# A small cast moved behind a split, other places for first weights, products in three passes, and a norm's small steps issued first

## The chip, the cores and the metric

The kernel runs on one core of one Trainium2 chip, as a single launch. The metric is the device time in microseconds (us) of the whole program; before the change it is 1896.98 us, the median of three runs.

## The reference

A decoder trunk of two layers over 512 tokens of width 1024, all in float32. Each layer is four blocks, each followed by a layer norm over the residual sum (a is a constant):

```python
x = layer_norm(a * x + 0.5 * swiglu_ffn(x, ffn_w_in[i, 0], ffn_w_out[i, 0]), ...)
h = diff_attention(...) if i == 0 else pool_mixer(...)
x = layer_norm(a * x + h, ...)
x = layer_norm(a * x + memory_cross_attention(x, mem, ...), ...)     # 256 memory tokens
x = layer_norm(a * x + 0.5 * swiglu_ffn(x, ffn_w_in[i, 1], ffn_w_out[i, 1]), ...)

def swiglu_ffn(x, w_in, w_out):          # w_in 1024 x 5632, w_out 2816 x 1024
    g, u = jnp.split(x @ w_in, 2, axis=-1)
    return (jax.nn.silu(g) * u) @ w_out
```

There are thus four feed-forward blocks, called blocks 1 to 4 below, and eight norms.

## The kernel before

Every float32 product is made of three matmuls. An operand is split into a high part (a cast on ACT, the ScalarE) and the rest (a subtraction on DVE, the VectorE): `xh`, `xl` for activations, `wh`, `wl` for weights. `mm3` multiplies high by high (L232), then L233 and L234 for the two mixed terms. The residual X stands in four tiles of 128 tokens, called X_76 to X_79 in the order of instructions; they are turned by TensorE through PSUM (`pt`), and cast and split into `xh` and `xl`.

A feed-forward block multiplies 2x2 blocks by seven products instead of eight. Its first half, `up()`, works on three column groups at a time ("lanes" 0, 1 and 2), in turns. A lane loads the raw weights `ra` and `rc` (later `rd`), some with an accumulating load issued on POOL, splits each in `operand()` (cast L769, subtraction L771), and makes the products x, y and z in PSUM; DVE combines them (L847) and ACT copies what has to be kept (`sp`, L832). A product that stands first for its block (`by_passes`, L796) takes 24 matmuls; before the change these are eight pairs on `xh` and `xl` with the weight's high part, and eight on `xh` with its low part.

A split weight lies in one of three kinds of place: the two turning buffers `wh`/`wl`, and two long places named `above` and `below`, which the mixers use too. `hl()` chooses by a counter:

```python
self.slot += self.by_fours
if self.by_fours and self.slot % 4 < 2:
    return self.long_place(self.slot % 2, shape, False)     # 0: above, 1: below
# else: the next buffer of wh and wl
```

The norm of a token tile (`ln_token`) is: partial sums with the residual on DVE (L397), mean on DVE (L406), Square with a running sum on ACT (L414), `var` on ACT (L415), `rstd` on POOL (L416), and two steps over the tile on DVE (L418, L420). `second_factors` then makes sums of turned tiles for the seven products (`hb`, L728 and L706).

The order on each engine is set by the order in the program text together with priorities (`high_priority`, `issue_after`, `behind`); each engine then runs its list in that order. `da_constants` prepares the attention's constants beside block 1: the mask is loaded by SP late, behind the block's last weights, cast to bfloat16 by DVE (L1829), and a gain is scaled (L1830). `left_over` is what remains of the last h's split in block 1 (L919 its low part).

Of the kernel before, what the change touches and what calls it, by code (L numbers as in the profile page):

```python
# [12 lines left out]
AF = mybir.ActivationFunctionType  # L13
ALU = mybir.AluOpType
# [4 lines left out]
D = 1024  # L19
S = 512  # L20
NT = S // P
# [6 lines left out]
EPS = 1e-5  # L28
# [4 lines left out]
LAM_INIT = 0.8 - 0.6 * math.exp(-0.3 * 0)  # L33
# [15 lines left out]
    scale=0.8,  # L49
# [78 lines left out]
class Trunk:  # L128
# [272 lines left out]
    def ln_token(self, t):  # L401
        nc, X = self.nc, self.X[t]
        g, b = self.ln_gb
        s = self.ln_sums[t]
        mean, var, rstd = (self.small(n, (P, 1)) for n in ("mean", "var", "rstd"))
        nc.vector.tensor_scalar(mean, s[:, 0:1], s[:, 1:2], -1.0 / D, ALU.add, ALU.mult)  # L406
        if self.last_ln:
            cols = [slice(half * S, (half + 1) * S) for half in range(2)]
        else:
            cols = [slice(0, D)]  # L410
        g, b = ([x[:, c] for c in cols] for x in (g, b))
        y = [X[:, c] for c in cols]
        sq = self.act(self.spare, (P, D), mybir.dt.bfloat16)
        square = nc.scalar.activation(sq, X, AF.Square, bias=mean, accum_out=var)  # L414
        nc.scalar.activation(var, var, AF.Copy, scale=1.0 / D, bias=EPS * self.ln_scale**2)  # L415
        nc.gpsimd.tensor_tensor(rstd, var, self.mhalf[:, 0:1], ALU.pow)  # L416
        for i, c in enumerate(cols):
            begin = nc.vector.scalar_tensor_tensor(y[i], X[:, c], mean, g[i], ALU.add, ALU.mult)  # L418
        for i, c in enumerate(cols):
            end = nc.vector.scalar_tensor_tensor(X[:, c], y[i], rstd, b[i], ALU.mult, ALU.add)  # L420
            if self.last_ln:
                nc.sync.dma_start(self.out[t * P : (t + 1) * P, c], X[:, c])
        self.ends.append((square, end))
        self.begins = square, begin
        self.passes.append(begin)
        if t == NT - 1:
            self.gates = list(self.next_gates)
        if self.make_xt:
            self.late.append(t)
# [157 lines left out]
    def ffn(self, layer, j, ln, beside=()):  # L587
        w_in, w_out = self.a["ffn_w_in"][layer, j], self.a["ffn_w_out"][layer, j]
        self.seven_of, self.factors = {}, self.factor_tiles()
        self.slot, self.by_fours, self.alike, self.urgent = 0, True, False, False  # L590
        nc, n, beside = self.nc, len(FFN_TURNS), iter(beside)
        at_start = bool(self.load_rest)
        downs = {i: self.down(d, w_out, 2.0 * ALPHA if i == 1 else 1.0) for i, (_, d) in enumerate(FFN_TURNS) if d}
# [152 lines left out]
    def up(self, w, u, lane, early, between):  # L746
# [5 lines left out]
        nc, H = self.nc, 2 * P  # L752
# [5 lines left out]
        def load(tag, *block):  # L758
            t = self.raw_tile((4, H), tag)
            self.last_load = nc.sync.dma_start(t, source(*block))  # L760
            return t
# [4 lines left out]
        def operand(raw, *behind):  # L766
            v = self.hl([P, 4, H])
            with self.after([act for act, _ in behind]):
                hi = nc.scalar.copy(v[0], raw)  # L769
            with self.after([dve for _, dve in behind]):  # L770
                lo = nc.vector.tensor_sub(v[1], raw, v[0].bitcast(F32))  # L771
            splits.append((hi, lo))
            return v

        def product(ps, v, a, start=False, passes=False):
            if passes or between and start and a == 0:
                by_passes(ps, v, a)
                return
            x = self.factors[a]
            for j in range(2):  # L780
                o = slice(j * P, (j + 1) * P)
                for k in range(4):

                    self.mm3(
                        ps[:, j], (v[0][:, k, o], v[1][:, k, o]), (x[0][:, k], x[1][:, k]),
                        start and j == k == 0, j == 1 and k == 3, True,
                    )

        def by_passes(ps, v, a, which=range(3)):

            x = self.factors[a]
            halves = [(n, i, l) for n in range(8) for i, l in ((0, 0), (0, 1))]
            for group in ([halves[:8], halves[8:], [(n, 1, 0) for n in range(8)]][w] for w in which):
                for n, i, l in group:
                    j, k = divmod(n, 4)
                    self.last_mm = nc.tensor.matmul(  # L796
                        ps[:, j], v[i][:, k, j * P : (j + 1) * P], x[l][:, k],
                        start=n == i == l == 0, stop=n == 7 and i == 1, skip_group_check=True,
                    )
# [5 lines left out]
        at_start = early > 0 and self.begins is None  # L805
# [7 lines left out]
        v = operand(ra, *((self.turned_parts,) if third and at_start else ()))  # L813
# [6 lines left out]
        if at_start and lane == 0:  # L820
            by_passes(x, v, 0, (0,))
            yield
# [4 lines left out]
        if at_start and lane == 0:  # L827
            by_passes(x, v, 0, (1, 2))
        else:
            product(x, v, 0, True, third and at_start)  # L830
# [19 lines left out]
        if not at_start or lane == 1:  # L850
            v = operand(ra)
            if u == FFN_LAST[1]:
                with self.tc.issue_after(splits[-1][1].ins):
                    self.left_over()
        elif third:
            v = operand(ra, self.made_parts, self.factor_parts)
        else:
            v = operand(ra, self.made_parts)
            self.made_parts = splits[-1]
            yield  # L860
# [6 lines left out]
        rd = load("rc", 2, 2)  # L867
# [3 lines left out]
        p5 = sp()  # L871
        nc.scalar.copy(p5, z)
        yield
        v = operand(rd)
        if at_start and lane == 0:
            self.made_parts = splits[-1]
            yield
# [14 lines left out]
        s = self.tmp("sp", (P, 2, H))  # L892
# [923 lines left out]
    def da_constants(self):  # L1816
        nc, a = self.nc, self.a
        c = lambda shape, name, dt=F32: self.ropep.tile(shape, dt, name=name)
        self.rope = c([P, 2], "rope")
        nc.sync.dma_start(self.rope, a["rope"])  # L1820
        self.ropeC, self.ropeS = c([P, S], "ropeC"), c([P, S], "ropeS")
        m = self.ropeC[:, :P]
        self.subg = c([P, 1], "subg")
        with self.tc.issue_after(self.last_load.ins):
            nc.sync.dma_start(m, a["mask"])
            nc.sync.dma_start(self.subg, a["da_subln_g"].rearrange("a p -> p a"))
        yield
        self.maskr = c([P, P], "maskr", mybir.dt.bfloat16)
        nc.vector.tensor_copy(self.maskr, m)  # L1829
        nc.vector.tensor_scalar(self.subg, self.subg, 1.0 - LAM_INIT, None, ALU.mult)  # L1830
        yield from self.rope_tables()


# [27 lines left out]
```

## Time and profile before

| | |
|---|---|
| median of three runs | 1896.98 us (1894.94 to 1900.29) |
| profiled execution, its own time | 1896.17 us |
| its span in the trace | 1894.4 us |
| busy: TensorE, its weight loads | 1880.5 us, 1779.3 us |
| busy: VectorE, ScalarE, GpSimd | 1546.9, 1000.6, 306.1 us |
| blocks 2, 3 and 4 begin near | 734, 1050, 1564 us |

Rows of the timeline give start, duration, engine, line, operation, output<-inputs and shapes; in brackets stands how long the engine was idle before it and what ended that. Rows of waits give the engine, line and tile, what it waited for, the total in us, how many times, and the longest. The names leave out buffer numbers.

### The profile page before, as it was taken

Reading aid. Unit: us, or ns where it says so; the run is one execution under the profiler, and the core shown is the slowest. Engines: PE = TensorE matmul, PEld = TensorE weight load, DVE = VectorE, ACT = ScalarE, POOL = GpSimd, SP = SyncE. Lnnn points to the kernel's source line nnn. Section 1 sums busy time; section 2 is a strip of 40 time slices with the busy share of each in tenths; the row PEclk is TensorE's granted clock in tenths of the full one; section 3 lists DMA queues with packets and bytes.
Section 4 is the critical chain, followed back from the end, with each engine's and each line's share of the span. In section 5 each row is a group of like instructions: output and inputs, shape, how many; then the busy total and the mean of one; then the engine's idle time right before and its main releaser. Section 6 shows DMA issues by size and latency. Waiting matters only on the chain.

```text
span 1894.4 us, 35092 instructions
## 1 busy us (share of the span) xinstructions
PE 1880.5 (99%) x14464; PEld 1779.3 (94%) x14464; DVE 1546.9 (82%) x2246; ACT 1000.6 (53%) x1542; POOL 306.1 (16%) x274
## 2 busy tenths in 40 slices
PE   9999999999999999999999999999999999999998
PEld 8999998888889988999999999999899889999997
DVE  7998889888877558898887989888786568998886
ACT  6555554566654435655554655455455436555552
POOL 3111120112110002221210311122120012111210
PEclk9999999999999999999999999999999999999999
DMA  9978872322235317978776688788464248877771
GB/s 253 226 168 169 188 130 90 103 68 72 95 112 178 112 64 183 189 167 181 159 160 191 110 172 188 166 175 160 163 173 149 97 122 164 182 163 172 164 149 56
DMA packets 250064, 283.36 MB, mean 150 GB/s; under 512 B 8752, under 2 KB 213040, under 8 KB 249904
## 3 DMA queue, kind: packets, MB, share of 16 engines
q0 software_dynamic: 94080, 94.38, 32.6%
q1 hardware_dynamic: 155824, 186.74, 30.4%
q8 instruction: 113, 1.85, 0.4%
q14 instruction: 47, 0.39, 0.1%
HBM read 274.79 MB, written 4.19 MB: 147 GB/s over the span
## 4 chain that ended last, share of the span: by engine, by line
PE 91%; DVE 3%; DMA 3%; ACT 1%; issue 1%; POOL 0%; SPq 0%; DVEq 0%; ACTq 0%; POOLq 0%
PE x L234 7%; PE x L232 7%; PE x L233 7%; PE z L234 4%; PE z L233 4%; PE z L232 4%; PE ps L232 4%; PE ps L233 4%; PE ps L234 4%; PE px L234 3%; PE px L232 3%; PE px L233 3%; PE x L796 3%; PE y L234 2%; PE y L232 2%; PE y L233 2%
## 5 line engine op out<-in xcount | busy, mean ns | idle before, releaser
L764 POOL DMA_DIRECT2D ra<-in_ffn_w_in_dram x132 | 171.5, 1359 | 1008.7 <-DVE wl L771 561.4
L769 ACT CAST wh<-ra 128x1024 fp32r<-128x1024 f32 x152 | 159.7, 1051 | 187.3 <-PE x L233 88.8
L771 DVE TENSOR_TENSOR wl<-ra,wh 128x1024 fp32r<-128x1024 f32 x152 | 184.6, 1223 | 32.5 <-ACT wh L769 30.8
L771 DVE TENSOR_TENSOR wl<-rc,wh 128x1024 fp32r<-128x1024 f32 x112 | 137.2, 1226 | 45.3 <-ACT wh L769 45.2
L769 ACT CAST wh<-rc 128x1024 fp32r<-128x1024 f32 x112 | 117.7, 1050 | 105.9 <-PE x L233 70.4
L232 PE MATMUL x<-xe,wh 128*128 128x256 f32 x608 | 168.0, 276 | 0.0
L234 PE MATMUL x<-xe,wl 128*128 128x256 f32 x608 | 168.0, 276 | 0.0
L233 PE MATMUL x<-xe,wh 128*128 128x256 f32 x608 | 168.0, 276 | 0.0
L232 PE MATMUL x<-xh,wh 128*128 128x256 f32 x472 | 130.9, 277 | 0.1
L233 PE MATMUL x<-xl,wh 128*128 128x256 f32 x472 | 130.7, 277 | 0.0
L234 PE MATMUL x<-xh,wl 128*128 128x256 f32 x472 | 130.5, 277 | 0.0
L145 DVE TENSOR_TENSOR wl<-raw,wh 128x1024 fp32r<-128x1024 f32 x64 | 78.6, 1236 | 47.9 <-ACT wh L144 47.3
L233 PEld LDWEIGHTS x<-xe,wh 128*128 128x128 f32 x608 | 114.2, 188 | 0.0
L234 PEld LDWEIGHTS x<-xe,wl 128*128 128x128 f32 x608 | 114.2, 188 | 0.0
L232 PEld LDWEIGHTS x<-xe,wh 128*128 128x128 f32 x608 | 114.2, 188 | 0.0
L144 ACT CAST wh<-raw 128x1024 fp32r<-128x1024 f32 x64 | 66.6, 1048 | 60.6 <-PE xq L233 18.8
L232 PEld LDWEIGHTS x<-xh,wh 128*128 128x128 f32 x472 | 88.7, 188 | 0.3 <-DVE X L397 0.3
L233 PEld LDWEIGHTS x<-xl,wh 128*128 128x128 f32 x472 | 88.7, 188 | 0.0
L234 PEld LDWEIGHTS x<-xh,wl 128*128 128x128 f32 x472 | 88.6, 188 | 0.0
L144 ACT CAST above<-b 128x1024 fp32r<-128x1024 f32 x60 | 63.1, 1052 | 44.0 <-PE pz L234 24.6
L234 PE MATMUL z<-xe,wl 128*128 128x256 f32 x312 | 86.2, 276 | 0.0
L233 PE MATMUL z<-xe,wh 128*128 128x256 f32 x312 | 86.2, 276 | 0.0
(557 smaller groups left out, 7156.0 us busy)
## 6 DMA issues: line engine op xcount, KB each, us to landing
ra<-in_ffn_w_in_dram POOLq DMA_DIRECT2D x132, 512.0 KB, 6.4
rc<-in_ffn_w_in_dram SPq DMA_DIRECT2D x88, 512.0 KB, 4.9
b<-in_ffn_w_out_dram SPq DMA_DIRECT2D x76, 512.0 KB, 4.4
ra<-in_ffn_w_in_dram SPq DMA_DIRECT2D x44, 512.0 KB, 5.6
rc<-in_ffn_w_in_dram POOLq DMA_DIRECT2D x44, 512.0 KB, 6.5
raw<-in_xa_wkv_dram SPq DMA_DIRECT2D x16, 1024.0 KB, 5.9
raw<-in_da_w_qkv_dram SPq DMA_DIRECT2D x24, 512.0 KB, 4.0
raw<-in_xa_wq_dram SPq DMA_DIRECT2D x8, 1024.0 KB, 5.4
```

The lines of the kernel that those rows point to most:

```text
L144: self.nc.scalar.copy(hi, src),
L145: self.nc.vector.tensor_sub(lo, src, hi.bitcast(F32)),
L232: self.first_mm = mm(out, w[0], x[0], start=start, stop=False, skip_group_check=again)
L233: mm(out, w[0], x[1], start=False, stop=False, skip_group_check=again)
L234: self.last_mm = mm(out, w[1], x[0], start=False, stop=stop, skip_group_check=again)
L764: nc.gpsimd.dma_start(t, source(*block), accum_op=ALU.add)
L769: hi = nc.scalar.copy(v[0], raw)
L771: lo = nc.vector.tensor_sub(v[1], raw, v[0].bitcast(F32))
L796: self.last_mm = nc.tensor.matmul(ps[:, j], v[i][:, k, j * P : (j + 1) * P], x[l][:, k], start=n == i == l == 0, stop=n == 7 and i == 1, s ...
```

## The change

Five edits. (1) `left_over` hands back its low split as `last_sums`, and the mask's cast and the gain's scaling are issued after it. (2) The place counter starts at 1 instead of 0 in blocks 2 to 4. (3) `by_passes` runs the first product in three passes: eight matmuls high by high, eight with `xl`, eight with the weight's low part. (4) In the norms not followed by a feed-forward block, and for the last token tile in all but the last norm, mean, Square, `var` and `rstd` are issued at high priority. (5) Lane 0's `rd` is split at high priority in the first turn of blocks 2 to 4.

```diff
         mean, var, rstd = (self.small(n, (P, 1)) for n in ("mean", "var", "rstd"))
-        nc.vector.tensor_scalar(mean, s[:, 0:1], s[:, 1:2], -1.0 / D, ALU.add, ALU.mult)
+        first = not self.last_ln and (t == NT - 1 or self.ln_next != "ffn")
+        with self.tc.high_priority() if first else nullcontext():
+            nc.vector.tensor_scalar(mean, s[:, 0:1], s[:, 1:2], -1.0 / D, ALU.add, ALU.mult)
...
-        square = nc.scalar.activation(sq, X, AF.Square, bias=mean, accum_out=var)
-        nc.scalar.activation(var, var, AF.Copy, scale=1.0 / D, bias=EPS * self.ln_scale**2)
-        nc.gpsimd.tensor_tensor(rstd, var, self.mhalf[:, 0:1], ALU.pow)
+        with self.tc.high_priority() if first else nullcontext():
+            square = nc.scalar.activation(sq, X, AF.Square, bias=mean, accum_out=var)
+        with self.tc.high_priority() if first else nullcontext():
+            nc.scalar.activation(var, var, AF.Copy, scale=1.0 / D, bias=EPS * self.ln_scale**2)
+            nc.gpsimd.tensor_tensor(rstd, var, self.mhalf[:, 0:1], ALU.pow)
...
-        self.slot, self.by_fours, self.alike, self.urgent = 0, True, False, False
+        self.slot, self.by_fours, self.alike, self.urgent = (0 if self.load_rest else 1), True, False, False
...
-            halves = [(n, i, l) for n in range(8) for i, l in ((0, 0), (0, 1))]
+            halves = [(n, 0, l) for l in range(2) for n in range(8)]
...
-                    self.left_over()
+                    self.last_sums = self.left_over()
...
-        v = operand(rd)
+        with self.tc.high_priority() if early > 1 and not at_start else nullcontext():
+            v = operand(rd)
...
-        nc.vector.tensor_copy(self.maskr, m)
-        nc.vector.tensor_scalar(self.subg, self.subg, 1.0 - LAM_INIT, None, ALU.mult)
+        with self.tc.issue_after(self.last_sums.ins):
+            nc.vector.tensor_copy(self.maskr, m)
+            nc.vector.tensor_scalar(self.subg, self.subg, 1.0 - LAM_INIT, None, ALU.mult)
```

The number of instructions on each engine stays the same. Line numbers of the code behind the norm move by 4 to 6: L414, L418 and L420 become L417, L422 and L424, L728 becomes L732, L769 and L771 become L773 and L775, L847 becomes L851, L919 becomes L924, L1829 becomes L1835.

VectorE near the end of block 1, before (`maskr` is the mask's copy, `subg` the gain, `hb<-sr,hb` the low split of h):

```order
L771 TENSOR_TENSOR wl<-rc,wh 128x1024
L1829 CAST maskr<-ropeC 128x128
L847 TENSOR_TENSOR hr<-y,sp 128x2x256
L1830 TENSOR_SCALAR subg<-subg 128x1
L771 TENSOR_TENSOR wl<-ra,wh 128x1024
L919 TENSOR_TENSOR hb<-sr,hb 128x1024
L847 TENSOR_TENSOR hr<-y,sp 128x2x256
L771 TENSOR_TENSOR wl<-ra,wh 128x1024
```

The same place on VectorE after:

```order
L775 TENSOR_TENSOR wl<-rc,wh 128x1024
L851 TENSOR_TENSOR hr<-y,sp 128x2x256
L775 TENSOR_TENSOR wl<-ra,wh 128x1024
L924 TENSOR_TENSOR hb<-sr,hb 128x1024
L851 TENSOR_TENSOR hr<-y,sp 128x2x256
L775 TENSOR_TENSOR wl<-ra,wh 128x1024
L1835 CAST maskr<-ropeC 128x128
L1836 TENSOR_SCALAR subg<-subg 128x1
```

The cast and the scaling went from ahead of the first `hr` and the first `wl<-ra` to behind the second `wl<-ra`.

VectorE at the start of block 2, before (the norm of the last token tile, X_79, between the first splits):

```order
L397 SCALAR_TENSOR_TENSOR X_79,sums<-X_79,ps 128x512
L771 TENSOR_TENSOR below<-ra,below 128x1024
L406 TENSOR_SCALAR mean<-sums 128x1
L418 SCALAR_TENSOR_TENSOR X_79<-X_79,mean,gb 128x1024
L771 TENSOR_TENSOR below<-rc,below 128x1024
L420 SCALAR_TENSOR_TENSOR X_79<-X_79,rstd,gb 128x1024
L771 TENSOR_TENSOR wl<-rc,wh 128x1024
```

The same place on VectorE after:

```order
L397 SCALAR_TENSOR_TENSOR X_79,sums<-X_79,ps 128x512
L775 TENSOR_TENSOR below<-rc,below 128x1024
L408 TENSOR_SCALAR mean<-sums 128x1
L775 TENSOR_TENSOR wl<-rc,wh 128x1024
L732 TENSOR_TENSOR hb<-pt,hb 128x4x128
L422 SCALAR_TENSOR_TENSOR X_79<-X_79,mean,gb 128x1024
L145 TENSOR_TENSOR xl<-hb,xh 128x4x128
L424 SCALAR_TENSOR_TENSOR X_79<-X_79,rstd,gb 128x1024
```

Lane 0's `ra` is no longer split here (its place is `wh`, and its split stands earlier); `rc`'s splits and the first `hb` went ahead of X_79's two steps.

ScalarE in the norm ahead of the attention, before (`sp,var<-X_79,mean` is the Square):

```order
L144 CAST xh<-pt 128x4x128 x2
L414 ACTIVATE sp,var<-X_79,mean 128x1024
L144 CAST wh<-raw 128x1024
L415 ACTIVATE var<-var 128x1
L144 CAST v<-v 128x4x128
```

The same place on ScalarE after:

```order
L144 CAST xh<-pt 128x4x128
L144 CAST wh<-raw 128x1024
L417 ACTIVATE sp,var<-X_79,mean 128x1024
L144 CAST xh<-pt 128x4x128
L419 ACTIVATE var<-var 128x1
L144 CAST v<-v 128x4x128
```

The weight's cast went from behind the Square to ahead of it, and the second cast of `xh` from ahead of it to behind it.

## The prediction

> **What bounds the kernel.** I read the page first: its totals, the granted clock, the chain.
>
> ```profile
> span 1894.4 us, 35092 instructions
> PE 1880.5 (99%) x14464; PEld 1779.3 (94%) x14464; DVE 1546.9 (82%) x2246; ACT 1000.6 (53%) x1542; POOL 306.1 (16%) x274
> PEclk9999999999999999999999999999999999999999
> PE 91%; DVE 3%; DMA 3%; ACT 1%; issue 1%; POOL 0%; SPq 0%; DVEq 0%; ACTq 0%; POOLq 0%
> ```
>
> TensorE is busy 1880.5 of 1894.4 us at full clock, and the chain runs 91% through it. The diff adds no matmul and takes none away, so it can win only out of the other 13.9 us, or lose by making TensorE wait where it doesn't now. Next I read all waits of TensorE.
>
> ```profile
> PE x L796 <- ACT below L769: 1.6, 2, 0.8
> PE idle L139 <- DVE hb L613: 1.2, 1, 1.2
> PE z L232 <- DVE subg L1830: 0.7, 1, 0.7
> PE z L234 <- DVE wl L771: 0.6, 1, 0.6
> PE x L796 <- DVE xl L145: 0.5, 1, 0.5
> PE pt L532 <- DVE X L420: 0.4, 1, 0.4
> ```
>
> Columns: total, times, longest. Left out are three rows of 0.5 (first 27 us), 0.2 and 0.2. One of the two waits in the first row, and the 1.2, lie in the first 9 us, where the weights are still arriving; the change doesn't reach them. The others stand at 253 (two), 342, 734 and 1565 us; I price the change there from the timeline. A start is late by its distance from the one before, less the usual 0.11 us (256 columns) or 0.23 (512).
>
> **Mask's cast.** The timeline at 250 to 256 us:
>
> ```profile
> 252.23 0.23 DVE L1829 CAST maskr<-ropeC 128x128 bf16<-128x128 f32 x1 [2.65 <-DMA ropeC<-in_mask_dram]
> 252.37 0.68 DVE L847 TENSOR_TENSOR hr<-y,sp 128x512 f32<-128x512 f32 x1
> 253.03 1.22 DVE L771 TENSOR_TENSOR wl<-ra,wh 128x1024 fp32r<-128x1024 f32 x1
> 249.78 1.05 ACT L769 CAST wh<-ra 128x1024 fp32r<-128x1024 f32 x1
> 252.25 0.28 PE L234 MATMUL y<-xh,wl 128*128 128x256 f32 x1
> 253.20 0.36 PE L232 MATMUL z<-xh,wh 128*128 128x256 f32 x1 [0.68 <-DVE subg L1830]
> 254.30 0.40 PE L234 MATMUL z<-xh,wl 128*128 128x256 f32 x1 [0.63 <-DVE wl L771]
> ```
>
> VectorE stands 2.65 us in front of a cast whose data are still on the way, and behind the cast wait L847 (which frees z's bank) and the low split of z's weight. z's first matmul comes 253.20 - 252.25 - 0.11 = 0.84 late, the third, 1.10 after it instead of 0.23, another 0.87. With the cast behind h's split, L847 can run as soon as its y is there, near 249.8 (24 matmuls of 0.113 before y's second lane ends at 252.36), and the split at 250.83, when ACT's cast is done, to 252.05. TensorE asks for them at 252.36 and 252.59. Both waits go: 1.71, taken as 1.7. Next in line is lane 1: L847 waits for its y until 252.4; behind h's split it ends at about 253.9, and its weight split at 255.0, against 255.3 where z's second lane needs it. Below 0.3 us of slack that would come back, hence a lower bound of 0.8; the upper is 1.9 with the short gaps of 0.1 behind. The cast's own reader is much later, in the attention. SP's loads keep their order here.
>
> **Lane 0's first weight, block 2.** The rows of 732 to 745 us:
>
> ```profile
> 732.60 0.39 PE L234 MATMUL ps<-kv,oT 128*128 128x512 f32 x1
> 733.79 0.39 PE L796 MATMUL x<-xh,below 128*128 128x256 f32 x1 [0.80 <-ACT below L769]
> 732.68 1.05 ACT L769 CAST below<-ra 128x1024 fp32r<-128x1024 f32 x1
> 737.58 0.21 DVE L406 TENSOR_SCALAR mean<-sums 128x1 f32<-128x1 f32 x1
> 739.16 1.28 DVE L418 SCALAR_TENSOR_TENSOR X<-X,mean,gb 128x1024 f32<-128x1024 f32 x1 [1.37 <-ACT p L414]
> 741.51 1.27 DVE L420 SCALAR_TENSOR_TENSOR X<-X,rstd,gb 128x1024 f32<-128x1024 f32 x1
> 744.30 0.71 PE L841 MATMUL y<-above 128*128 128x512 f32 x2
> ```
>
> `below` is cast only after the cross attention lets it go, so x starts 1.19 - 0.23 = 0.96 late. `wh` is free well before, so x starts at 732.83 and its 24 matmuls end 0.96 sooner, plus 0.19 for a second short gap. But token tile 79's transposes come ahead of y: L420 ends at 742.78 and is ready now 0.73 before they start at 743.51. In the new order a split and a copy of hb go ahead of X_79's two steps, into the 1.37 us in which VectorE idled: from the mean's end at 737.79, a split (1.2) and the copy (0.6) give 739.6 for the first step; it ends at 740.8, one xl later the second runs from 741.4 to 742.6. TensorE would be there at 742.3 to 742.5. So about 0.2 of the 1.15 is lost again: 0.9, bounds 0 and 1.15. The third lane's accumulating load goes ahead of X_79's rstd on POOL; its issue, at 738.2 before, ends before var is there: nothing. Two loads change places on SP, both with their places free: nothing.
>
> **Three passes.** They count in block 4:
>
> ```profile
> 1564.97 0.39 PE L796 MATMUL x<-xl,below 128*128 128x256 f32 x1 [0.47 <-DVE xl L145]
> 1569.21 1.29 DVE L418 SCALAR_TENSOR_TENSOR X<-X,mean,gb 128x1024 f32<-128x1024 f32 x1 [1.65 <-ACT p L414]
> 1574.55 1.22 DVE L771 TENSOR_TENSOR above<-rc,above 128x1024 fp32r<-128x1024 f32 x1
> 1575.58 0.28 PE L233 MATMUL y<-xl,above 128*128 128x256 f32 x1
> 1575.82 0.39 PE L234 MATMUL y<-xh,above 128*128 128x256 f32 x1
> ```
>
> The second matmul wanted xl and came 0.63 late; eight matmuls on xh alone, 0.91 us, cover that, and 0.2 of small gaps. But VectorE's list from X_79's mean to rc's split is the same as before, it starts from a Square whose mean comes from the block's own last sums, and y's third matmul already waits for that split (0.24 instead of 0.11). Whatever x saves, y waits: I take 0.1, bounds 0 and 0.85. Block 3 has no wait to lose; the weight's cast that now stands ahead of X_79's Square waits there for the first 16 matmuls, some 0.6 us, inside the norm's slack: nothing, bounds 0.3 either way.
>
> **Norm's small steps.** The attention's norm, 338 to 343 us, and rstd:
>
> ```profile
> 338.19 1.15 ACT L414 ACTIVATE sp<-X,mean 128x1024 bf16<-128x1024 f32 x1
> 341.19 1.29 DVE L420 SCALAR_TENSOR_TENSOR X<-X,rstd,hr 128x1024 f32<-128x1024 f32 x1 [0.44 <-POOL rstd L416]
> 341.84 0.28 PE L234 MATMUL v<-wh,xl 128*128 128x256 f32 x1
> 342.54 0.44 PE L532 MATMUL pt<-ident,X 128*128 128x128 f32 x2 [0.42 <-DVE X L420]
> L416 POOL TENSOR_TENSOR rstd<-var,mhalf x31: 539/1079/1665, 316.5 to 1881.1; 128x1 f32<-128x1 f32 x31
> 726.34 1.35 POOL L416 TENSOR_TENSOR rstd<-var,mhalf 128x1 f32<-128x1 f32 x1 [3.15 <-ACT var L415]
> 725.99 1.28 DVE L418 SCALAR_TENSOR_TENSOR X<-X,mean,gb 128x1024 f32<-128x1024 f32 x1 [0.77 <-ACT p L414]
> ```
>
> X_79's transposes are 0.59 late. In the new order its mean goes ahead of an xl, but ACT now has a `wh<-raw` cast ahead of the Square, so the Square starts near 338 to 338.5, about as before, if that weight is there by 337 (its load follows the split of an earlier one, which the new order does sooner). VectorE fits an xl between the two steps: the second ends near 342.3 instead of 342.48. I take 0.2, bounds 0.6 gained and 0.3 lost. A rstd that starts inside the first step takes 1.35 us instead of 0.54 and ends 0.42 after that step; with an xl (0.69) or an hb in between, as in the new order of all these places, that costs nothing.
>
> The Trainium skill's page "SBUF — State Buffer", section "SBUF: two separate sides", has a rule that speaks against the early rstd: VectorE and GpSimd share a port pair under an exclusive lock, so a GpSimd instruction can be held for a whole VectorE instruction. The spread of 539 to 1665 ns agrees. If rstd lost its turn to one more instruction in block 2 and in the attention's norm, both gains there would go, and the sum would be 1.7 instead of 2.8.
>
> In the cross attention's norm X_78's first sums go behind X_77's two steps, close to where their bank is needed again: -0.1, bounds -0.2 and 0. The pooling's norm: 0. Lane 0's rd split moves ahead; it stood here:
>
> ```profile
> 759.91 1.23 DVE L771 TENSOR_TENSOR wl<-rc,wh 128x1024 fp32r<-128x1024 f32 x1
> 761.20 0.28 PE L232 MATMUL z<-xe,wh 128*128 128x256 f32 x1
> 108.20:110.92 2.72, 2.72 (x26) 2.72 (x25) 2.52 (x4) 2.05 (x3) 0.00 (x0) 1.00 1.04 304
> 116.36:119.08 2.72, 2.72 (x26) 2.72 (x25) 2.34 (x4) 1.05 (x1) 0.00 (x0) 1.00 0.79 235
> ```
>
> It ends 0.07 before its product starts and nothing waits: 0. The swap of `above` and `below` in the rest of blocks 2 to 4 is free too: the last two rows are 24 px matmuls out of `above` and 24 out of `below`, 2.72 us each.
>
> **Sum.** 1.7 + 0.9 + 0.1 + 0.2 - 0.1 = 2.8 us. The profiled execution took 1896.17 us, 0.81 below the median of 1896.98: 1893.4 by the one and 1894.2 by the other, so 1893.8. The bounds add to between 0.0 and 4.8 gained. 0.3% is 5.7 us, about what a measurement of this kernel tells from no change.
>
> **Rivals.** (1) All waits go and nothing takes their place: 1.71 + 1.15 + 0.85 + 0.59 = 4.3 us, some 1892.3. For it: the norm's chains get slack of their own by the earlier small steps. Against: block 4's list on VectorE is unmoved. (2) The norms' chains set every end: only the mask's 1.7 are left, 1895.0; for it block 4's row of y; the port rule gives this result too. (3) Slower. In the first turn of blocks 2 to 4 VectorE is full (row after row in 758 to 762 without a gap), and the rd split at its new place pushes another step, a factor or the third lane's ra split, past the matmul that reads it. A split with its cast is 1.22 + 1.05 = 2.27 us, in three blocks 6.8: 1896.6 - 2.8 + 6.8 = 1900.6. It decides from 0.93 us in each. Against it: in block 2 the order gains 1.3 us of VectorE's idle time first, and adding up the new order's rows from 742.6 I find the third lane's split done at 757.2, 0.6 before its use. (4) The cast moves, but the split behind L847 still comes late, held by something that the mask's wait hid: then 0.84 of the 1.7 is left, 1894.7.
>
> **Chances.** Forecast 0.55, (1) 0.15, (2) 0.13, (3) 0.08, (4) 0.04, anything else 0.05. Of (1), which falls 1.4 short of 5.7 us, a good half could still be measured as faster, since runs of one kernel spread by 5 us (1894.94 to 1900.29 before), and so could some of the forecast's and the unnamed: faster 0.16; (3): slower 0.08; same 0.76. The range for 8 in 10 takes in the bounds and 1.5 us of that spread: 1890.3 to 1897.8.
>
> **What will show it.** Right if the waits on subg and the wl at 253 are gone and VectorE's wait for the mask lies behind the second wl<-ra; if x in block 2 starts 0.23 behind the last ps, with X_78's transposes or X_79's waiting a few tenths; if block 4's y waits nearly a microsecond for rc's split; and if busy TensorE stays at 1880. Wrong if new waits on wl, xe or hb appear after the first products of blocks 2 to 4, or if those y's wait for nothing.

## The result, and the profile after

The changed kernel takes 1892.13 us (median of 10 runs, 1891.49 to 1896.37), the kernel before 1896.38 us beside it (10 runs, 1894.51 to 1900.29). The ratio is 0.9978, 95% interval 0.9969 to 0.9986: about 4.2 us faster, 0.22%, within the 0.3% that the prediction called no change, and 1.7 us below the predicted 1893.8. One run of e1 (2686 us), one of e9 (1937 us) and one of the kernel before beside e9 (4887 us), all far above the rest, are left out of the medians and ratios below.

The profiled execution of the changed kernel took 1893.81 us, 2.4 less than that of before; its page and all waits of TensorE:

```profile
span 1892.0 us, 35088 instructions
PE 1881.3 (99%) x14464; PEld 1781.2 (94%) x14464; DVE 1548.6 (82%) x2246; ACT 1003.4 (53%) x1542; POOL 308.3 (16%) x274
```

```profile
PE idle L139 <- DVE hb L617: 1.2, 1, 1.2
PE y L800 <- ACT wh L773: 0.4, 1, 0.4
PE x L800 <- DVE below L775: 0.3, 1, 0.3
PE x L800 <- ACT below L773: 0.3, 1, 0.3
PE pt L536 <- DMA X<-in_x_dram: 0.2, 1, 0.2
PE po L1290 <- DVE a L145: 0.2, 1, 0.2
```

All but the last row lie in the first 27 us, while the weights arrive. The waits at 253, 342, 734 and 1565 us are gone. But TensorE's busy time went up by 0.8 us with the same 14464 matmuls: some of them ran slower, and that is the second half of the story. First the places, in the timeline of the changed kernel. The mask's:

```profile
250.56 0.69 DVE L851 TENSOR_TENSOR hr<-y,sp 128x512 f32<-128x512 f32 x1 [0.26 <-PE y L234]
251.58 1.23 DVE L775 TENSOR_TENSOR wl<-ra,wh 128x1024 fp32r<-128x1024 f32 x1 [0.32 <-ACT wh L773]
254.46 1.22 DVE L775 TENSOR_TENSOR wl<-ra,wh 128x1024 fp32r<-128x1024 f32 x1
255.59 0.22 DVE L1835 CAST maskr<-ropeC 128x128 bf16<-128x128 f32 x1
253.08 0.28 PE L232 MATMUL z<-xh,wh 128*128 128x256 f32 x1
253.20 0.28 PE L233 MATMUL z<-xl,wh 128*128 128x256 f32 x1
253.31 0.28 PE L234 MATMUL z<-xh,wl 128*128 128x256 f32 x1
```

The first hr runs as soon as its y is there, the weight's split follows when ACT's cast is done, z's three kinds of matmul follow each other at 0.11 us, and the cast finds its data. The start of block 2 (TensorE's rows, then VectorE's and GpSimd's):

```profile
730.90 0.40 PE L234 MATMUL ps<-kv,oT 128*128 128x512 f32 x1
731.13 0.88 PE L800 MATMUL x<-xh,wh 128*128 128x256 f32 x6
735.51 1.21 DVE L775 TENSOR_TENSOR wl<-rc,wh 128x1024 fp32r<-128x1024 f32 x1
737.25 1.27 DVE L422 SCALAR_TENSOR_TENSOR X<-X,mean,gb 128x1024 f32<-128x1024 f32 x1
738.44 0.68 DVE L145 TENSOR_TENSOR xl<-hb,xh 128x512 fp32r<-128x512 f32 x1
739.04 1.28 DVE L424 SCALAR_TENSOR_TENSOR X<-X,rstd,gb 128x1024 f32<-128x1024 f32 x1
737.31 1.61 POOL L420 TENSOR_TENSOR rstd<-var,mhalf 128x1 f32<-128x1 f32 x1 [6.51 <-ACT var L419]
```

x follows the last ps by 0.23 us, as forecast. rstd starts inside VectorE's first step over the tile and takes 1.61 us instead of 0.54, which fits the lock of the Trainium skill's page "SBUF — State Buffer" ("SBUF: two separate sides"); the xl between the two steps hides it, so it costs nothing in this execution.

The attention's norm, VectorE's rows:

```profile
337.77 1.29 DVE L422 SCALAR_TENSOR_TENSOR X<-X,mean,hr 128x1024 f32<-128x1024 f32 x1 [1.50 <-ACT sp L417]
338.97 0.69 DVE L145 TENSOR_TENSOR xl<-pt,xh 128x512 fp32r<-128x512 f32 x1
339.57 1.28 DVE L424 SCALAR_TENSOR_TENSOR X<-X,rstd,hr 128x1024 f32<-128x1024 f32 x1
```

The second step directly follows the xl; the transposes come 0.35 behind the matmul ahead of them, where it was 0.70.

**A second pace.** In block 2's first turn the kernels do the same matmuls, and nothing waits in either. Columns: window, length, TensorE's busy time and number of matmuls, granted clock, two on DMA. The window from 760 to 790 us in the kernel before, then in the changed one:

```profile
760.00:790.00 30.00, 30.00 (x268) 1.00 1.12 224
```

```profile
760.00:790.00 30.00, 30.00 (x257) 1.00 1.05 215
```

The clock is granted in full in both, and yet 257 matmuls run where 268 did: from start to start it is 117.8 ns instead of 113.3 for 256 columns. In the changed kernel's execution the slow pace lasts, but for short breaks, from the cross attention until 801 us, and some 500 matmuls there cost 2.2 us. That is about what its profiled gain of 2.4 us falls short of the 4.2 by the medians.

### The profile page after: what moved, and what is told of

Same layout as the page of the kernel before. It is cut to its first block, busy times and chain, and to the rows that moved or that the text cites. A ratio compares the mean times of both kernels' runs of the same rounds, so it can differ in the third digit from the quotient of the medians.

```text
span 1892.0 us, 35088 instructions
## 1 busy us (share of the span) xinstructions
PE 1881.3 (99%) x14464; PEld 1781.2 (94%) x14464; DVE 1548.6 (82%) x2246; ACT 1003.4 (53%) x1542; POOL 308.3 (16%) x274
## 4 chain that ended last, share of the span: by engine, by line
PE 97%; DMA 1%; DVE 1%; ACT 1%; SPq 0%; issue 0%; POOL 0%; DVEq 0%; POOLq 0%; ACTq 0%
PE x L233 7%; PE x L234 7%; PE x L232 7%; PE ps L232 5%; PE ps L234 5%; PE ps L233 5%; PE z L233 4%; PE z L234 4%; PE z L232 4%; PE px L233 3%; PE px L234 3%; PE px L232 3%; PE x L800 3%; PE y L233 2%; PE y L232 2%; PE y L234 2%
## 5 line engine op out<-in xcount | busy, mean ns | idle before, releaser
L773 ACT CAST wh<-ra 128x1024 fp32r<-128x1024 f32 x149 | 156.6, 1052 | 185.6 <-PE x L233 89.3
L775 DVE TENSOR_TENSOR wl<-ra,wh 128x1024 fp32r<-128x1024 f32 x149 | 180.8, 1221 | 33.2 <-ACT wh L773 31.2
L773 ACT CAST wh<-rc 128x1024 fp32r<-128x1024 f32 x115 | 120.9, 1051 | 119.6 <-PE x L233 74.1
L775 DVE TENSOR_TENSOR wl<-rc,wh 128x1024 fp32r<-128x1024 f32 x115 | 140.5, 1222 | 49.8 <-ACT wh L773 49.7
L232 PE MATMUL x<-xe,wh 128*128 128x256 f32 x632 | 174.6, 276 | 0.0
L233 PE MATMUL x<-xe,wh 128*128 128x256 f32 x632 | 174.6, 276 | 0.0
L232 PE MATMUL x<-xh,wh 128*128 128x256 f32 x424 | 117.4, 277 | 0.0
L234 PE MATMUL x<-xh,wl 128*128 128x256 f32 x424 | 117.2, 276 | 0.0
L233 PE MATMUL x<-xl,wh 128*128 128x256 f32 x424 | 117.2, 276 | 0.0
L975 DVE SCALAR_TENSOR_TENSOR X<-X,px 128x512 f32<-128x512 f32 x128 | 85.0, 682 | 1.4 <-PE px L234 1.4
L144 ACT CAST below<-b 128x1024 fp32r<-128x1024 f32 x58 | 61.0, 1053 | 46.1 <-PE pz L234 24.6
L420 POOL TENSOR_TENSOR rstd<-var,mhalf 128x1 f32<-128x1 f32 x31 | 35.3, 1137 | 300.1 <-ACT var L419 300.1
L232 PE MATMUL y<-xh,wh 128*128 128x256 f32 x304 | 84.0, 276 | 0.0
L233 PE MATMUL y<-xl,wh 128*128 128x256 f32 x304 | 84.0, 276 | 0.0
L234 PE MATMUL y<-xh,wl 128*128 128x256 f32 x304 | 84.0, 276 | 0.0
```

Of the source, the lines that this page charges most:

```text
L144: self.nc.scalar.copy(hi, src),
L232: self.first_mm = mm(out, w[0], x[0], start=start, stop=False, skip_group_check=again)
L233: mm(out, w[0], x[1], start=False, stop=False, skip_group_check=again)
L234: self.last_mm = mm(out, w[1], x[0], start=False, stop=stop, skip_group_check=again)
L975: nc.vector.scalar_tensor_tensor(X, X, by, ps, ALU.mult, op)
```

## The experiments

Four kernels with one edit each, then further executions of the changed kernel and versions of it. The fifth edit, the earlier split of `rd`, has no run of its own. From each profiled execution I took these stretches of TensorE, in us: from the start of the y ahead of the mask's place to the px behind z, and to the first ps of the block's end; from the v ahead of X_79's transposes to these transposes in the attention's norm; from the last ps to the first y of block 2 (its 512-column matmuls counted as y), and to the first px of block 2; the same to the first y of block 4.

| execution | mask to px | mask to ps | attention's norm | block 2 to y | block 2 to px | block 4 to y |
|---|---|---|---|---|---|---|
| before | 12.87 | 48.23 | 0.70 | 11.71 | 66.68 | 10.93 |
| changed | 10.88 | 46.24 | 0.35 | 10.40 | 67.48 | 10.30 |
| mask only (e1) | 10.88 | 46.24 | 0.70 | 11.68 | 68.76 | 10.30 |
| places only (e2) | 12.54 | 49.29 | 0.70 | other order | 66.62 | 10.30 |
| passes only (e3) | 12.96 | 49.71 | 0.70 | 11.69 | 66.67 | 10.30 |
| norm only (e4) | 12.82 | 48.18 | 0.35 | 11.58 | 66.60 | 10.30 |
| changed (e5) | 10.88 | 46.24 | 0.31 | 11.16 | 68.24 | 10.30 |
| changed (e6) | 10.88 | 46.24 | 0.60 | 10.67 | 65.62 | 10.30 |
| without places (e7) | 10.88 | 46.24 | 0.45 | 11.03 | 66.80 | 10.30 |
| changed (e9) | 10.88 | 46.24 | 0.59 | 10.58 | 67.66 | 10.30 |
| without mask (e11) | 12.76 | 48.12 | 0.41 | 10.65 | 67.73 | 10.30 |
| without mask (e12) | 12.95 | 49.69 | 0.34 | 10.64 | 65.60 | 10.30 |

### Mask only

```diff
-        nc.vector.tensor_copy(self.maskr, m)
-        nc.vector.tensor_scalar(self.subg, ...)
+        with self.tc.issue_after(self.last_sums.ins):
+            nc.vector.tensor_copy(self.maskr, m)
+            nc.vector.tensor_scalar(self.subg, ...)
```

> Only the mask's cast and the gain's scaling go behind h's split; the other four edits are left out. Theory: both waits at 253 us vanish and nothing takes their place, so TensorE is 1.7 to 2.0 us ahead of the kernel before from 260 us to the end, about 1894.5 us. Rival: lane 1's split comes too late and a part comes back, 0.8 us ahead. On the matmul pace in block 2's first turn (113 ns per 256 columns in the kernel before from 745 to 801 us, 118 in the changed one): if the pace follows the missing wait at block 2's start, it is 113 here, since that wait is still there; if it changes by chance from run to run, it may be either.

1895.4 us against 1897.59 (9 and 31 runs), ratio 0.9981 (0.9971 to 0.9991). The place takes 10.88 us instead of 12.87: 1.99, both waits gone, nothing late next. In block 2 x still waited (it starts 1.08 us behind the last ps), and yet the pace there was slow to the end of the turn, 68.76 us to px: a wait at x doesn't ensure the fast pace.

### Places only

```diff
-        self.slot, ... = 0, True, False, False
+        self.slot, ... = (0 if self.load_rest else 1), True, False, False
```

> Only the counter's start (1 instead of 0 in blocks 2 to 4). Theory: x in block 2 starts 0.23 us behind the last ps, a gain of about 1.3 us there as in the changed kernel; in block 4 the third lane's ra is split ahead of X_76's sums, not between them, so VectorE's norm chain is 0.9 us ahead of the kernel before, while TensorE still waits some tenths for xl. Rival: block 4's chain is as in the kernel before, and its gain came from the three passes or the norm's steps. Pace in block 2's first turn: 118 if it follows the missing wait at the start of x, 113 or 118 if by chance. Time: 1895.0 with the pace of before, 1897 with 118.

1896.57 us, ratio 0.999 (0.9981 to 1.0): 1.0 us by the medians, 1.9 by the ratio, with an interval that reaches no change. x starts 0.23 behind the last ps. But without the norm's early steps X_79's norm holds TensorE; the scheduler has put seven matmuls of y ahead of its transposes, and these wait:

```profile
PE pt L536 <- DVE X L424: 1.4, 2, 1.0
```

The longer one is the new wait, in block 2 (the other, 0.4, is the attention's). It eats the 0.96 won at x: with the pace fast, px comes after 66.62 us, in the kernel before after 66.68. So in this execution the places alone give nothing in block 2; with the norm's steps beside them and the fast pace, e6 and e12 get to px after 65.62 and 65.60. Block 4's gain is not from the places either: 10.30 us stands in every other row too.

### Passes only

```diff
-            halves = [(n, i, l) for n in range(8) for i, l in ((0, 0), (0, 1))]
+            halves = [(n, 0, l) for l in range(2) for n in range(8)]
```

> Only the order of the first products' matmuls (eight, eight, eight). Theory from the prediction: in block 4 the wait for xl of 0.6 us goes, but y waits about 0.9 us longer for rc's split, net 0.1 us. Rival: the wait goes and y waits for nothing, net 0.85 us, since the norm's chain has room. The block's first matmuls at 24 to 27 us: if the 0.7 us that the changed kernel is behind there comes from the three passes at the start, it is seen here too; if from the loads of that one execution, not. Pace in block 2's first turn: 113 if it follows the wait at its start. Time: 1896.3.

1897.24 us, ratio 0.9996 (0.9987 to 1.0005): no change that can be measured. Both theories on block 4 fell: the wait for xl that the order was to cover is absent in e1, e2 and e4 too, which have the old order. What differs is one late weight in the one profiled execution of before. ScalarE's rows there, and the same three casts with the same code in e1:

```profile
1542.79 1.05 ACT L769 CAST below<-ra 128x1024 fp32r<-128x1024 f32 x1 [1.66 <-DMA ra<-in_ffn_w_in_dram]
1544.23 1.05 ACT L769 CAST wh<-ra 128x1024 fp32r<-128x1024 f32 x1 [0.38 <-DMA ra<-in_ffn_w_in_dram]
1547.60 1.05 ACT L769 CAST wh<-ra 128x1024 fp32r<-128x1024 f32 x1 [2.32 <-DMA ra<-in_ffn_w_in_dram]
```

```profile
1545.50 1.05 ACT L773 CAST below<-ra 128x1024 fp32r<-128x1024 f32 x1 [1.75 <-DMA ra<-in_ffn_w_in_dram]
1546.92 1.05 ACT L773 CAST wh<-ra 128x1024 fp32r<-128x1024 f32 x1 [0.37 <-DMA ra<-in_ffn_w_in_dram]
1548.41 1.05 ACT L773 CAST wh<-ra 128x1024 fp32r<-128x1024 f32 x1 [0.44 <-DMA ra<-in_ffn_w_in_dram]
```

The third weight landed 1.9 us later, its split on VectorE stood ahead of X_76's last sums, and the whole norm behind it was 0.94 late, down to the xl that x waited for. As to the first 27 us: e3 shows no loss there, so the three passes don't explain the 0.7 us of the changed kernel's execution.

### Norm only

```diff
+        first = not self.last_ln and (t == NT - 1 or self.ln_next != "ffn")
+        with self.tc.high_priority() if first else nullcontext():     # mean, Square, var, rstd
```

> Only the norm's small steps at high priority (mean, Square, var, rstd); lane 0's rd split is left at its old priority. Theory: 0.4 us at the attention's norm (342 us) and 0.4 to 0.5 at the pooling's (1407 us), nothing in blocks 2 to 4, so about 1895.5 us. Rival: the attention's norm gains only with the other places, and the pooling's wait for wl stays, so 1896.4 us. Pace in block 2's first turn: 113 if it follows the wait at its start, either if by chance.

1896.41 us, ratio 0.9996 (0.9986 to 1.0005). The attention's norm gives 0.35 us; the pooling's wait for wl, 0.38 late in the execution of before, is 0.06 here, but 0.26 in e3 and none in e2, so it changes from execution to execution without these edits too. By its time the kernel can't be told from no change.

### The changed kernel again

> The changed kernel itself, a second profiled execution. What is asked is the matmul pace in block 2's first turn (745 to 801 us). Theory: TensorE takes one of two paces, 113 or 118 ns per 256 columns, and keeps it until a matmul waits a little; with no wait at block 2's start the slow pace that the cross attention always ends with is carried on to 801 us: 118 again, about 2 us lost, span near 1892. Rival: the pace there is chance in each execution: 113 this time or in the next look.

> The changed kernel itself, a third profiled execution. Theory (the pace is carried on where nothing waits): 118 ns in 745 to 801 us once more, and no slow stretch behind 257 us, since nothing waits there any more. Rival (chance): 113 in one of the two looks.

1895.69 and 1892.63 us (one execution each). The slow pace was carried on in neither: in e5 it ended at 736 us and began again at 742, in e6 it ended at 735 and stayed away. Where it ended, X_78's transposes came 0.33 and 0.37 us behind the matmul ahead of them instead of 0.12, so a short wait may have ended it, as the theory allows. But a wait doesn't decide: e9, e11 and e12 have about the same gap there and one of 0.25 at X_79's transposes, and from there to px e9 and e11 are slow and e12 is fast. So the pace is settled anew in each execution.

To px block 2 took 68.24 us in e5 and 65.62 in e6, against 66.68 before: with the fast pace the edits win 1.06 there. From the first y to px it is 57.08 in e5 and 54.95 in e6, so the slow pace takes 2.1 away; the other 0.5 of e5 is X_79's norm, and the slow pace began behind it (rows of TensorE, GpSimd and VectorE):

```profile
741.87 0.28 PE L234 MATMUL x<-xh,above 128*128 128x256 f32 x1
742.63 0.55 PE L536 MATMUL pt<-ident,X 128*128 128x128 f32 x3 [0.49 <-DVE X L424]
739.04 2.22 POOL L420 TENSOR_TENSOR rstd<-var,mhalf 128x1 f32<-128x1 f32 x1 [6.51 <-ACT var L419]
740.17 0.68 DVE L145 TENSOR_TENSOR xl<-hb,xh 128x512 fp32r<-128x512 f32 x1
741.29 1.29 DVE L424 SCALAR_TENSOR_TENSOR X<-X,rstd,gb 128x1024 f32<-128x1024 f32 x1 [0.44 <-POOL rstd L420]
```

Here rstd took 2.22 us, not 1.61, and ended 0.41 behind the xl, where in the other three executions of this kernel it ended 0.4 behind the first step. This is the case that the prediction names: rstd lost its turn to one more of VectorE's instructions, the xl no longer hid it, and VectorE and then TensorE waited.

And TensorE waits in the cross attention, near 722 us, for the sums of the norm there. In e9 this is longest:

```profile
PE ps L232 <- DVE X L397: 0.6, 1, 0.6
```

The 60 matmuls up to the last ps take 12.48, 12.36 and 12.78 us in e5, e6 and e9, but 11.87 in the first execution: 12.4 in the mean of the four. In the five with the old places they take 11.97 (before), 11.87 (e1, e7), 11.88 (e4) and 12.28 (e3), 12.0 in the mean. So 0.4 us is lost there on average; what makes the wait come and go wasn't found.

### Without the places

```diff
-        self.slot, ... = (0 if self.load_rest else 1), True, False, False
+        self.slot, ... = 0, True, False, False
```

> The changed kernel with the counter starting at 0 in every block, the other four edits kept. Theory: x in block 2 waits 1 us for its cast again; that costs 1.0 to 1.3 us, and in about three of four executions the wait ends the slow pace, which gives 2 us back: so equal to or up to 1 us faster than the changed kernel, 1891 to 1892. Rival: the pace has nothing to do with it and the kernel is 1.3 us slower than the changed one, about 1893.5, with 118 and 113 seen alike.

1894.47 us, ratio 0.9985 (0.9975 to 0.9995), against 0.9978 for the changed kernel: 1.3 us slower by the ratios, the rival's number, but the intervals overlap and the two weren't timed side by side. The wait at x is back:

```profile
PE x L800 <- ACT below L773: 1.3, 2, 1.0
```

Two waits, of which the shorter is block 2's (0.3; x starts 0.65 behind the last ps), the other lies in the first 27 us. That is 0.42 late, not 0.96 as in the kernel before. There ScalarE did the cast straight behind a cast of xh:

```profile
732.22 0.57 ACT L144 CAST xh<-pt 128x512 fp32r<-128x512 f32 x1
732.68 1.05 ACT L769 CAST below<-ra 128x1024 fp32r<-128x1024 f32 x1
```

In e7 both casts come 0.54 us sooner against the last ps (the cast of `below` 0.46 ahead of it, where it was 0.08 behind), and x by as much. `below` was free by then, so how late x starts hangs also on how far ScalarE has come in its list. To y block 2 took 11.03 us in e7 and 10.70 in the mean of the four executions of the changed kernel; to px 66.80 and 67.25. The traces thus don't show the 1.3 us in block 2.

### Without the two 512-column matmuls

```diff
-            if early > 1 and not at_start:
-                wide = v2[0][:, :2].rearrange("p k n -> p (k n)")
-                for _ in range(2):
-                    nc.tensor.matmul(y..., v2[0][:, 0, :P], wide, start=True, stop=True)
             product(y, v2, 1, True, lane != 1 and at_start)
```

> The changed kernel without the two 512-column matmuls ahead of y in blocks 2 to 4 (their result is overwritten by y, so the outputs stay). Theory: y's operands are there 0.5 us early in all three blocks (in block 4 just so), so each block gains up to 0.55 us, 1.0 to 1.6 us in all. Rival: VectorE is full in those turns, and the later products wait for what y gained: no change. Both: y then starts straight behind transposes, which may also leave the pace at 118 longer (blocks 3 and 4 lose up to 2 us each).

> The changed kernel once more, timed beside the next three on one chip. Theory: 0.997 to 0.998 of the kernel before, about 1893, with a spread of 1 to 4 us from stretches at the slow matmul pace. In the trace X_79's transposes in block 2 wait 0 to 0.5 us and the rest of the first turn runs at 113 or 118, by chance.

> The changed kernel without the two 512-column matmuls ahead of y in blocks 2 to 4, timed beside the changed kernel itself. Theory: 0.5 us per block, 1.4 us faster than the changed kernel (1.37 us of matmuls leave the stream: six at 0.228), with the same chance of slow stretches. Rival: the 512-column matmuls help to end the slow pace that follows the transposes, and without them block 4 (slow from 1563 to 1630 us in the first look) and others lose 1 to 3 us in part of the executions: equal in the median, with a wider spread.

First 1891.9 us, ratio 0.997 (0.9959 to 0.998, 8 runs). Timed side by side: the changed kernel (e9) 1893.6 us, 0.998 (0.9971 to 0.9989); without those matmuls (e10) 1891.9 us, 0.9974 (0.9965 to 0.9983); 10 and 11 runs, before 1897.0. That is 1.7 us by the medians and 1.1 by the ratios, but the intervals overlap. It has the lowest ratio of the versions. Both theories are half right. In e8 and e10 the first px of block 3 comes after 64.79 us instead of 65.27, and that of block 2 after 65.14 and 65.13, less than in any other execution. But in block 4 it comes after 67.00 instead of 65.27, in both: the slow pace that follows the transposes goes on to px there, while in blocks 2 and 3 it ends without the two matmuls. The window from 1585 to 1615 us in e9 and in e10:

```profile
1585.00:1615.00 30.00, 30.00 (x267) 1.00 1.12 209
```

```profile
1585.00:1615.00 30.00, 30.00 (x257) 1.00 1.12 230
```

None of the 12 other executions is slow there. Keeping the two matmuls in block 4 alone might give these back; it wasn't tried.

### Without the mask's move

```diff
-        with self.tc.issue_after(self.last_sums.ins):
-            nc.vector.tensor_copy(self.maskr, m)
-            nc.vector.tensor_scalar(self.subg, ...)
+        nc.vector.tensor_copy(self.maskr, m)
+        nc.vector.tensor_scalar(self.subg, ...)
```

> The changed kernel with the mask's cast at its old place, the other four edits kept. Theory: the two waits at 253 us are back, 1.7 to 2.0 us; and a short wait of z's second lane at 257 us is back too (0.02 us), after which the pace is slow to 297 us in about half of the executions, 1.5 us more: 2.5 us slower than the changed kernel on average. Rival: only the waits count, 1.7 us slower.

> A second look at the same kernel as the one above, for the pace behind 257 us: slow (118 ns) from 257 to 297 us in this look or the other by the theory; if both are fast, the slow stretches there in two executions so far had another cause than that wait.

1894.67 us, ratio 0.9989 (0.998 to 0.9998), against 0.998 for the changed kernel beside it (e9): 1.0 us by the medians, 1.7 by the ratios. That is nearer to the waits alone, but the intervals are too wide to tell 1.7 from the theory's 2.5. The trace does show a second effect. The window behind the mask's place in e11 and e12, two executions of one kernel:

```profile
262.00:288.00 26.00, 26.00 (x232) 1.00 0.73 139
```

```profile
262.00:288.00 26.00, 26.00 (x223) 1.00 0.77 144
```

Of the six executions with the cast at its old place, three are slow until 297 us, e2 and e3 from 257, e12 from 254, straight behind the two waits: to ps they take 49.29 to 49.71 us, the three others 48.12 to 48.23. With the cast moved it is 46.24 in all eight (e8 and e10 too). So the move is worth 1.9 to 2.0 or 3.1 to 3.5 us in an execution, 2.6 in the mean of these six. That the waits bring the slow stretch on fits three in six against none in eight, but isn't shown beyond that.

## Why the prediction came out right

The forecast was 2.8 us of gain; measured were 4.2, and 3.3 in the second timing (e9). Range and direction held, and the terms that carry the sum were found where they were looked for. Step by step:

- Mask's cast: forecast 1.7, upper bound 1.9; it is 1.99 to px, because besides the short gaps counted z's second lane lost one of 0.14. The slack named for what is next in line held: lane 1's split ends at 255.68, in time. What the bound left out is the slow stretch that followed the old waits in half of the executions; with it the term is 2.6, 0.9 more than forecast.
- Lane 0's first weight: forecast 0.9, bounds 0 and 1.15. The four executions of the changed kernel reach the first y 1.31, 0.55, 1.04 and 1.13 us sooner than before, 1.0 in the mean. That X_79's norm takes a part back was right as a mechanism: e2 shows how large that part is without the norm's steps, and e5 what a late rstd does, 0.5. But this gain doesn't last to px: there the four need 67.25 us in the mean, the five executions with the old places (before, e1, e3, e4, e7) 67.10. And of x's 0.96 in the kernel before, 0.54 is missing in e7 with the places unchanged, so the place let go late is not the whole of that wait.
- Three passes in block 4: forecast 0.1, and the step failed in its premise. I read the wait for xl as a property of the kernel; it was one late load in one execution, and so were the 0.85 of rival (1) and the row of y's wait. The edit gives nothing there. In the difference of the two profiles it stands as 0.86. With this a sign that the prediction had named as wrong came true: y waits for nothing in block 4, where it was to wait nearly a microsecond for rc's split. Only 0.1 of the sum hung on it.
- Attention's norm: forecast 0.2, bounds -0.3 to 0.6; 0.35, 0.39, 0.10 and 0.11 in the four executions. The condition named was the right one: in e6 and e9 the weight's cast that now stands ahead of the Square waited 0.25 for its load. Cross attention: forecast -0.1, bounds -0.2 and 0; the wait near 722 us costs 0.4 in the mean, beyond the bound. Pooling: forecast 0, and nothing that stands out from the chance there. Block 3: forecast 0; its way to y is 10.30 us in every execution with the 512-column matmuls.
- The swap of `above` and `below`, priced at nothing by two windows of px: no execution speaks against it. But equal windows were taken as proof that a matmul has one price, and it has two. In block 2's first turn three of the four executions of the changed kernel ran slow and lost there more than they had won at its start.
- Rivals: the first timing is nearest to (1)'s 4.3 of gain, the second lies between it and the forecast; no wait that it counts is left in the first profile, as it says, but block 4's 0.85 of it were no gain of the edits. (3) and (4) are out: the kernel isn't slower, no wait on wl, xe or hb appears behind the first products, and both of the mask's waits went. (2), the mask's part alone, is out for the way to y in block 2 and for the attention's norm; by the times it isn't, once the mask's part is 2.6.

Counted with the slow stretches, the terms are 2.6 for the mask, -0.15 for block 2 to px, 0.25 for the attention's norm and -0.4 for the cross attention's, 2.3 us in all. That is near the forecast's 2.8 in part by luck: the mask's term was too small by about as much as block 2's was too large. The measured 4.2 has an interval of 2.7 to 5.9 us (0.9986 and 0.9969 of 1896.4), the second timing one of 2.1 to 5.5 (0.9989 and 0.9971 of 1897.0). So the terms lie near the lower end of both, and where the rest of the median's gain comes from is open.

## What to carry to other kernels

A stall list from one execution mixes waits that the program makes with waits that one late transfer made: before a price is put on a wait of half a microsecond, look at what released it, and if a DMA stands at the head of that chain, look at a second execution. An instruction that waits for late data should stand in its engine's list behind all work that others need; a quarter microsecond of cast cost 2.0 us here (1.99 in e1). And where a place is freed sooner, the next thing in line (here a norm of four small steps) has to be moved with it, or the gain is waited away, as in e2.

## What the runs showed of the hardware

TensorE has two paces at the same granted clock of 1.00: 113.3 and 117.8 ns from start to start for 256 columns, 4.5 ns more for each matmul. A stretch lasts from some twenty to several hundred matmuls; it begins and ends near transposes, at the first px of a turn, or at a matmul that waited, and the same place in the same kernel goes either way (e11 and e12 behind 257 us). The Trainium skill's page "TensorE: Matmul & The Clock Gate", section "Back-to-back issue gap", has one gap for isolated matmuls on a warm array, N / 2.4 + 2.5 ns, which is an estimate of 109 ns for 256 columns; neither pace is that. Its clock gate isn't what tells the two paces apart, since the granted clock is full in both. For 512 columns there are no such two groups: the long stretches here average 227 to 234 ns. Counting 4.5 ns for every 256-column matmul at 116 ns or more, slow stretches cost some 5 to 10 us in an execution, so that a good part of the 5 us by which runs of one kernel differ may come from them. The four executions of the changed kernel stand in the same order by this cost as by their span (e6, the first, e9, e5: 1890.9, 1892.0, 1893.0 and 1893.9 us). What sets the pace is open.
